# Diffusion backbone with routed experts: splits inside the rare branch, a sort spread over partitions, earlier transposes in experts, and ones multiplied during modulation

## The chip, the cores and the metric

The kernel runs on one core of a Trainium2 chip, which has engines that each run their own stream of instructions: TensorE (PE, matmuls), VectorE (DVE), ScalarE (ACT), GpSimd (POOL) and SyncE (SP, which issues most transfers). They wait for each other by semaphores. The metric is device time of one execution in microseconds (us); a number is the median of several executions.

## The reference

One layer of a hybrid backbone on 1024 tokens of width 1024: a modulation vector from the condition, a mixer (attention, recurrence, short convolution), and a mixture of 16 experts in which each token is routed to two. What bears on the change:

```python
mod = (cond @ w_ada[l] + b_ada[l]).reshape(bsz, N_MOD, 1, D_MODEL)
h = modulate(rms_norm(x, norm_mix_g[l]), mod[:, 0], mod[:, 1])
...
for e in range(N_EXPERTS):
    hid = jax.nn.silu(h @ w_gate[e]) * (h @ w_up[e])
    out = out + combine[..., e:e + 1] * (hid @ w_down[e])
```

Gate and up weights of an expert are 1024 x 512 each, the down weight 512 x 1024.

## The kernel before

**Precision.** Every float32 operand of a matmul is split into two parts of lower precision, `hi` (a cast by ACT) and `lo` (raw minus `hi`, by DVE), and a product is three matmuls (hi x hi, lo x hi, hi x lo). For a weight that is `Weights.split` (line 1756 for the DVE part, 1755 for ACT's): an expert's weights are 12 pieces of 128 x 1024, eight for gate and up (one for each 128 rows of the width) and four for down. `need(w, n)` splits until n pieces are done, `fill()` splits one more piece wherever it stands, up to 12 per expert and as far as buffers are free.

**Modulation at the start.** For j = 0 to 7 `weigh(j)` forms weighted sums of `w_ada` columns on ACT, DVE and POOL, and `total(j)` (lines 228 to 238) adds them up on PE: for each of two halves, two small matmuls on `wa` (line 233) and then two with ones on `mc` (line 235). `mods` reads the result on DVE (242, 244). `turn` transposes normalized tokens on PE (251), and ACT and DVE apply the modulation to them (254 to 256). `steps` (334) multiplies them by the input projection.

**Experts.** Tokens are sorted into lists in memory, one per expert. All experts have a first tile of 128 tokens (`Tile`, matmuls into `pg`). Experts 0 and 1 are taken in fixed places and are of kind "I": if they have more than 128 tokens, a branch (`tc.If(n > P)`, line 1591) runs `later`. The other 14 are sorted by their counts (`places`), and six of them, at places 2, 4, 6, 8, 10 and 12, are of kind "H" and have a half tile of 64 tokens besides (`Half`, `ph`). The rest have one tile. A few tokens beyond that are done in a tail.

The loop of one expert: `gate_up` for the first 4 of 8 slices of the width in both halves of the hidden width; the If of experts 0 and 1; the half tile's `gate_up`; the remaining slices; `act` (tanh on ACT, line 1364, and two operations on DVE, 1365 and 1366, make `t`); `Tile.turn`, which transposes `t` (PE 1389) and splits it into `hT` (ACT 1391, DVE 1392); transposes of the next expert's gathered tokens (`turn(xgs[0], 0)`, PE 1346, then ACT 92 and DVE 93 make `xT`); `down` (PE 1400); and `store`, in which DVE scales the result into `yt` (1405) for a scatter by POOL. The half tile does the same by lines 1414, 1416 (PE), 1427 (ACT), 1428 (DVE), 1438 (transposes on PE), 1441 (ACT), 1442 (DVE) and 1455.

**The order.** Each engine runs its instructions in the order in which this code issues them; nothing reorders them. So an operation on ACT or DVE stands behind all splits that `need` and `fill` put ahead of it. Memory in SBUF and PSUM is taken from pools with a fixed number of buffers: a new tile waits until the last reader of the old one is done.

Before the loop, expert 0's tokens come straight from PSUM (`xp`), are split into `xT` half by half, the lists of experts 0 and 1 are looked up by the ACT queue (`look`), and `places` sorts on one partition. In experts 0 and 1 all 12 pieces are split before the If, since both sides of it use them:

```python
                if KINDS[i] == "I":
                    need(w, 12)
                    with tc.If(n > P):
                        later(i, n, w)
```

Of the kernel before, what the change touches and what calls it, by code (L numbers as in the profile page):

```python
# [18 lines left out]
P = 128  # L19
D = 1024  # L20
# [14 lines left out]
C_ID, C_TRI, C_II, C_I16, C_GRP, C_E, C_TIE, C_POS, C_HALF, C_CAP, C_N = (  # L35
    0, 128, 256, 320, 336, 352, 368, 382, 396, 397, 411)
# [35 lines left out]
class Kernel:  # L72
# [84 lines left out]
    def start(self):  # L157
# [3 lines left out]
        with self.pool("xp", side="right") as xp:  # L161
# [46 lines left out]
            mt = [self.mo.tile([P, D], F32, name=c, bufs=n).rearrange("p (q i f) -> p q i f", i=2, f=P)  # L208
                  for c, n in (("macc", 1), ("mw", 2))]
# [18 lines left out]
            def total(j):  # L228

                pm = self.pmm.tile([P, 2, 2], F32, name="pm")  # L230
# [52 lines left out]
            for j in range(1, KD + 1):  # L283
                if 1 < j < KD - 2:
                    weigh(j + 2)
                if j < KD:
# [4 lines left out]
                if j == 1:  # L291
                    weigh(3)
                if j < KD:
# [30 lines left out]
    def steps(self, i, g, k0, k1):  # L324

        o, n = (0, 512, 1024)[g], (512, 512, 256)[g]
        if k0 == 0:
# [36 lines left out]
    def inproj(self, hc_es):  # L364
# [93 lines left out]
        def norm(ys, base):  # L458
# [8 lines left out]
            pn = self.pmm.tile([P, 8], F32, name="pm")  # L467
# [544 lines left out]
    def mixout(self):  # L1012
# [237 lines left out]
        V.tensor_copy(cn, pc[0:1, :])  # L1250
# [18 lines left out]
    def places(self, buf):  # L1269

        V, cst, cn, N = self.V, self.cst, self.cn, NE - 2
        dn, key, rk = (buf[0:1, 16 * i:16 * i + n] for i, n in enumerate((NE, N, N)))
        g1, g2 = (buf[0:1, i:i + N * N].rearrange("o (p e) -> o p e", e=N) for i in (256, 512))
        fix = lambda c: cst[0:1, c:c + N]
        inner, outer = (lambda x: x[:, None, :].to_broadcast([1, N, N])), (lambda x: x[:, :, None].to_broadcast([1, N, N]))
        V.scalar_tensor_tensor(out=key, in0=cn[:, 2:], scalar=16.0, in1=fix(C_TIE), op0=ALU.mult, op1=ALU.add)
        V.tensor_tensor(out=g1, in0=inner(key), in1=outer(key), op=ALU.is_gt)
        V.tensor_reduce(out=rk, in_=g1, axis=AX.X, op=ALU.add)
        V.tensor_tensor(out=g1, in0=inner(rk), in1=outer(fix(C_POS)), op=ALU.is_equal)
        V.tensor_tensor(out=g2, in0=g1, in1=inner(fix(C_I16 + 2)), op=ALU.mult)  # L1280
# [567 lines left out]
```

## Time and profile before

| | |
|---|---|
| median of 3 runs | 1118.6 us (1116.49 to 1125.67) |
| the profiled execution's own time | 1112.07 us |
| its span | 1110.3 us |
| PE busy | 1006.4 us (91%), 5242 instructions |
| DVE busy | 820.9 us (74%) |
| ACT busy | 592.5 us (53%) |
| POOL busy | 305.5 us (28%) |
| mean granted clock of PE | 0.977 |

The span is the profiled part of an execution. Busy is the time in which an engine executes; an engine waits for data in the rest, or has nothing to do. [...] The start (modulation) ends at about 75 us, and the experts run from 678 to about 1057 us.

### The profile page before, as it was taken

What the parts mean: (1) busy time and instruction counts of PE and PEld (TensorE: products, weight loads), DVE (VectorE), ACT (ScalarE), POOL (GpSimd) and SP (SyncE); (2) the same over time, 40 slices, a digit from 0 to 9 for tenths busy, and PEclk for the clock granted to TensorE, in tenths of its full rate; (3) what the DMA queues carried; (4) which work ended last, traced back from release to release, by engine and by line L of the source; (5) the groups of instructions that cost most, each with busy time, mean ns of one, the idle gap of its engine ahead of it and who ended that gap; (6) DMA issues with size and microseconds to landing.
All of it is one profiled execution on the core that took longest, in us unless ns stands there. A gap on an engine that the chain in (4) does not pass through costs nothing. (4 is left out here: it accounts for less than half of the span.)

```text
span 1110.3 us, 15751 instructions
## 1 busy us (share of the span) xinstructions
PE 1006.4 (91%) x5242; PEld 821.0 (74%) x5243; DVE 820.9 (74%) x1415; ACT 592.5 (53%) x964; POOL 305.5 (28%) x212
## 2 busy tenths in 40 slices
PE   2699999989999879998899996899999999999994
PEld 2577778878888779987788875677777777777773
DVE  5886897734563358887676777789797979889965
ACT  6674683432332358887422224567574756656751
POOL 3630012220001125245213233131323334131431
PEclk9999999989999989999999989899999999999997
DMA  9441434779444677775676747988998979898873
GB/s 326 137 124 61 144 93 120 260 258 311 143 133 120 176 192 197 239 204 191 249 265 226 275 143 270 362 273 270 308 293 272 326 247 340 236 351 246 286 254 133
DMA packets 139595, 251.21 MB, mean 226 GB/s; under 512 B 25283, under 2 KB 87205, under 8 KB 139460
## 3 DMA queue, kind: packets, MB, share of 16 engines
q1 hardware_dynamic: 130804, 228.13, 62.5%
q0 software_dynamic: 6736, 19.53, 7.4%
q10 hardware_dynamic: 1968, 2.47, 0.7%
q8 instruction: 45, 0.74, 0.3%
q14 instruction: 42, 0.34, 0.1%
HBM read 211.94 MB, written 45.55 MB: 232 GB/s over the span
## 5 line engine op out<-in xcount | busy, mean ns | idle before, releaser
L334 PE MATMUL ps<-h,block 128*128 128x512 f32 x1056 | 255.6, 398 | 2.1 <-DVE block L321 1.2
L334 PEld LDWEIGHTS ps<-h,block 128*128 128x128 f32 x1056 | 198.7, 191 | 44.1 <-DVE block L321 2.2
L1380 PE MATMUL pg<-q,xT 128*128 128x512 f32 x448 | 136.7, 398 | 3.4 <-DVE xT L93 2.7
L1380 PE MATMUL pg<-k,xT 128*128 128x512 f32 x320 | 112.3, 405 | 3.0 <-PEq L1591 2.8
L1336 POOL DMA_INDIRECT acc_d<-yt,recs x15 | 69.3, 4621 | 125.4 <-DVE yt L1405 125.4
L1380 PEld LDWEIGHTS pg<-q,xT 128*128 128x128 f32 x448 | 84.5, 189 | 24.6 <-DVE xT L93 2.8
L1756 DVE TENSOR_TENSOR q<-block,k 128x1024 fp32r<-128x1024 f32 x80 | 94.9, 1217 | 2.7 <-ACT k L1755 1.2
L1400 PE MATMUL py<-k,hT 128*128 128x512 f32 x204 | 81.2, 435 | 10.3 <-DVE hT L1392 4.2
L1755 ACT CAST k<-block 128x1024 fp32r<-128x1024 f32 x80 | 80.2, 1047 | 4.1 <-DMA recs<-list_d 3.8
L733 POOL TENSOR_TENSOR bt<-bt,mask 128x768 f32<-128x768 f32 x32 | 58.9, 1852 | 84.0 <-DMA bt<-b_d 83.9
L1380 PEld LDWEIGHTS pg<-k,xT 128*128 128x128 f32 x320 | 61.0, 191 | 17.5 <-issue 2.9
L782 ACT ACTIVATE sm<-sm,mx 128x640 f32<-128x640 f32 x64 | 53.2, 831 | 19.5 <-DVE mx L774 19.1
L796 DVE TENSOR_TENSOR p<-ps,p 128x640 fp32r<-128x640 f32 x64 | 52.6, 821 | 12.2 <-ACT p L795 12.1
L1400 PEld LDWEIGHTS py<-k,hT 128*128 128x128 f32 x204 | 40.0, 196 | 28.0 <-DVE hT L1392 10.7
L774 DVE CUSTOM_DVE_ANT_0 sm<-ps,bt 128x640 f32<-128x640 f32 x64 | 52.2, 817 | 9.8 <-PE ps L770 7.5
L770 PE MATMUL ps<-k,q 128*128 128x384 f32 (+1 forms) x256 | 52.6, 329 | 5.4 <-DVE q L703 2.2
L793 PE MATMUL ps<-cst,sm 128*128 128x128 f32 x320 | 47.0, 278 | 7.6 <-DVE mx L774 6.8
L520 DVE SCALAR_TENSOR_TENSOR macc<-mw,sil,macc 128x1024 f32<-128x1024 f32 x28 | 37.7, 1347 | 20.8 <-DMA mw<-in_w_ada_dram 20.6
L795 ACT CAST p<-ps 128x640 fp32r<-128x640 f32 x64 | 44.3, 692 | 16.1 <-PE ps L793 15.5
L1297 POOL DMA_INDIRECT block<-h_d,recs x21 | 26.3, 1252 | 94.5 <-PE pt L1346 75.8
L770 PEld LDWEIGHTS ps<-k,q 128*128 128x128 f32 x256 | 43.3, 194 | 7.4 <-issue 2.4
L98 POOL TENSOR_TENSOR ms<-ms,cst 128x1 f32<-128x1 f32 x26 | 17.5, 679 | 105.4 <-DVE ms L97 85.4
(373 smaller groups left out, 2278.3 us busy)
## 6 DMA issues: line engine op xcount, KB each, us to landing
block<-in_w_moe_dram SPq DMA_DIRECT2D x120, 512.0 KB
raw<-in_w_moe_dram SPq DMA_DIRECT2D x36, 512.0 KB
mw<-in_w_ada_dram SPq DMA_DIRECT2D x32, 512.0 KB
k<-in_w_moe_dram SPq DMA_DIRECT2D x24, 512.0 KB
bt<-b_d SPq DMA_DIRECT2D x30, 384.0 KB
block<-in_w_in_dram SPq DMA_DIRECT2D x22, 512.0 KB
wa<-in_w_ada_dram SPq DMA_DIRECT2D x16, 512.0 KB
block<-v_d SPq DMA_DIRECT2D x64, 128.0 KB
```

Of the source, the lines that this page charges most:

```text
L334: self.E.matmul(ps[:, 0:n], l[:, k, :], r[:, m, :], start=(k == 0 and q == 0), stop=(k == KD - 1 and q == 2))
L733: self.G.tensor_add(out=v, in0=v, in1=self.masks[n][:, g:g + 1].to_broadcast([P, 2, 384]))
L770: E.matmul(ps[:, dst], self.qs[i][h][:, it * P:(it + 1) * P], kv, start=(i == 0), stop=(i == 1))
L774: V.tensor_tensor_reduce(out=sm, in0=ps[:, all_], in1=self.bts[(u // 2) % 2][:, g, b0:b0 + 640], op0=ALU.add, op1=ALU.min, scale=-1.0, sca ...
L782: S.activation(sms[u, g], sms[u, g], AF.Exp, scale=-1.0, bias=mx, accum_out=lss[n][:, g, h:h + 1])
L793: E.transpose(pt[:, b * P:(b + 1) * P], sm[:, c:c + P], ident)
L796: return lambda: V.tensor_sub(pl, pt, ph.bitcast(F32))
L1336: nc.gpsimd.indirect_dma_start(out=acc_d, out_offset=bass.IndirectOffsetOnAxis(ap=rec[0:m, 1:2], axis=0), in_=y[0:m], in_offset=None, comp ...
L1380: E.matmul(self.pg[half], self.xT[x][:, k, :], self.w.gu(k, m, half), start=(k == 0 and i == 0), stop=(k == KD - 1 and i == 2))
L1400: E.matmul(self.py[c], hTs[x][:, f, :], self.w.dn(f, m, c), start=(f == 0 and i == 0), stop=(f == 3 and i == 2))
L1755: k.S.copy(hi, raw)
L1756: (eng or k.V).tensor_sub(lo, raw, hi.bitcast(F32))
```

## The change

- **Modulation.** A tile of ones (`one`, cast once by POOL) is multiplied by itself in `warm(n)`, matmuls whose result nobody reads: 8 in total(0) and 20 in total(1), between the `wa` and the `mc` matmuls of the first half, 5 ahead of the transposes of j == 1, 8 at j == 2. The PSUM tile `pm` becomes a whole bank.
- **Rare branch.** In experts 0 and 1 the If comes after 12 matmuls (first half, slices 0 to 3) and with 4 pieces split; `later` splits the other 8 for itself. On the usual side they are split where `fill` and `need` stand. Expert 0's two ACT copies now come ahead of both DVE subtractions, and its third terms stand last. In expert 1 the half transposes for `later` come ahead of the first matmuls.
- **Sort.** `places` works on 16 partitions, one per expert, in two parts with two small matmuls between; the first part runs in expert 0 ahead of `need(w, 8)`, the second after `act(1)`. The look at expert 2 follows it. Record loads of experts 0 and 1 go to POOL's queue.
- **Experts with a half tile.** `t.turn(1)` comes right after the half tile's first half; the next tokens are transposed in two groups of four with matmuls between; `t.store(c)` comes ahead of `h.turn(c)`.

```diff
+            def warm(n, t=None):
+                for _ in range(n):
+                    E.matmul(self.acc[0, 0] if t is None else t, one[:, 0:P], one[:, 0:512], start=True, stop=True)
...
+                    if i == 0:
+                        warm({0: 8, 1: 20}.get(j, 0))
...
+                if j == 1:
+                    warm(5)
...
+                if j == 2:
+                    warm(8, self.pmm.tile([P, 512], F32, name="pm"))
...
+        total = lambda x, y, out: V.tensor_tensor_reduce(out=sc, in0=x, in1=y, op0=ALU.mult, op1=ALU.add, scale=1.0, scalar=0.0, accum_out=out)
+        V.scalar_tensor_tensor(out=key, in0=self.lc[0:NE, 2:NE], scalar=16.0, in1=fix(C_TIE), op0=ALU.mult, op1=ALU.add)
+        total(key, fix(C_ID + 2), own)
+        V.tensor_tensor(out=sc, in0=key, in1=own.to_broadcast([NE, N]), op=ALU.is_gt)
+        V.tensor_reduce(out=rk, in_=sc, axis=AX.X, op=ALU.add)
+        V.tensor_scalar(oh, fix(C_POS), rk, None, op0=ALU.is_equal)
...
+        yield
+        pt = pst.tile([P, 512], F32, name="pt")[0:1]
+        E.matmul(pt[:, 0:N], cst[0:NE, C_IX:C_IX + 1], oh, start=True, stop=True)
+        E.matmul(pt[:, NE:2 * NE], dn, cst[0:NE, C_ID:C_ID + NE], start=True, stop=True)
...
-                    self.load(recs[:, i], lv[expert[i], :, 0:2], self.S if i < 2 else None)
+                    self.load(recs[:, i], lv[expert[i], :, 0:2], self.G if i < 2 else None)
...
+                done, m = list(w.parts), 12 - len(w.parts)
+                assert min(len(w.raw), len(self.his), len(self.los)) >= m
+                for hi, lo, raw in zip(self.his[:m], self.los[:m], w.raw):
+                    self.split(hi, lo, raw)
+                    w.parts.append((hi, lo))
...
                 if KINDS[i] == "I":
-                    need(w, 12)
+
+                    t.gate_up(0, 0, 4, not i)
                     with tc.If(n > P):
                         later(i, n, w)
+                    if not i:
+                        fill(2)
+                    gate_up(t, 1, 0, 4, 1 + (not i))
...
                 w.release(4)
+                if not i:
+                    order = self.places(yt, pst)
+                    next(order)
                 need(w, 8)
...
+                if not i:
+                    next(order, 0)
+                    look(2)
                 if half:
                     h.gate_up(0, 4)
+                    t.turn(1)
                     fill()
                 ahead(i + 2)
                 if i:
-                    x0 = turn(xgs[0], 0)
+                    x0 = turn(xgs[0], 0, (0,))
+                    if half:
+                        h.act(0)
+                        h.gate_up(1, 4, 6)
+                    turn(xgs[0], 0, (1,))
                     gather(rec(i + 2, 0), xgs[0]) if i + 2 < NE else None
                 if half:
-                    h.act(0)
-                    h.gate_up(1, 4)
+                    h.gate_up(1, 6)
                     fill()
-                    t.turn(1)
                     h.act(1)
...
                         t.down(c, 1)
+                        t.store(c)
                         h.turn(c)
-                        t.store(c)
```

Lines of the changed kernel stand 10 to 44 higher than those of before. Three places, each before and after.

DVE around the If of expert 0, before: after the end of the sort (1291 to 1293) come eight splits and the branch.

```order
L1293 CAST cnts<-yt 1x1
L1582 TENSOR_LOAD cnts
L1756 TENSOR_TENSOR q_4754<-block_5137,k_4753 128x1024
L1756 TENSOR_TENSOR q_4823<-block_5138,k_4822 128x1024
L1756 TENSOR_TENSOR q_4884<-block_5139,k_4883 128x1024
L1756 TENSOR_TENSOR q_4943<-block_5140,k_4942 128x1024
L1756 TENSOR_TENSOR q_4988<-block_5141,k_4987 128x1024
L1756 TENSOR_TENSOR q_5030<-block_4608,k_5029 128x1024
L1756 TENSOR_TENSOR q_5038<-block_4609,k_5037 128x1024
L1756 TENSOR_TENSOR lo<-block_4610,hi 128x1024
L1591 COMPARE_AND_BRANCH
```

After, behind the If: the last of four splits, the first part of the sort (1290 to 1295; two rows of 1290 make one operation), two splits and the first operation on `t`.

```order
L1802 TENSOR_TENSOR q_4986<-block_5183,k_4985 128x1024
L1291 SCALAR_TENSOR_TENSOR yt<-lc,cst 16x14
L1290 ISA yt<-yt,cst 16x14
L1290 ISA yt 16x1
L1293 TENSOR_TENSOR yt<-yt 16x14
L1294 TENSOR_REDUCE yt<-yt 16x1
L1295 TENSOR_SCALAR yt<-cst,yt 16x14
L1290 ISA yt<-yt,cst 16x14
L1290 ISA yt 16x1
L1802 TENSOR_TENSOR q_5031<-block_5184,k_5030 128x1024
L1802 TENSOR_TENSOR q_5073<-block_4651,k_5072 128x1024
L1386 SCALAR_TENSOR_TENSOR t_6302<-t_6302,pg_6359 128x256
```

The eight splits moved behind the branch; `t` stands behind six of them and the first part of the sort, where it stood behind all eight, two more and the whole sort.

PE in expert 2 (a half tile), before: the half tile's first half ends (`ph_7151`), then eight transposes of the next tokens and the second half (`ph_7160`); `t_6260`, the second half of the first tile, is transposed after it.

```order
L1414 MATMUL ph_7151<-q_4943,xT_6252 64x512
L1416 MATMUL ph_7151<-k_4942,xT_6252 128x512
L1346 MATMUL pt<-cst,block_5452 128x128 x8
L1414 MATMUL ph_7160<-q_4754,xT_6252 64x512
L1416 MATMUL ph_7160<-k_4753,xT_6252 128x512
L1414 MATMUL ph_7160<-q_4823,xT_6252 64x512
L1416 MATMUL ph_7160<-k_4822,xT_6252 128x512
L1414 MATMUL ph_7160<-q_4884,xT_6252 64x512
L1416 MATMUL ph_7160<-k_4883,xT_6252 128x512
L1414 MATMUL ph_7160<-q_4943,xT_6252 64x512
L1416 MATMUL ph_7160<-k_4942,xT_6252 128x512
L1389 MATMUL pt<-cst,t_6260 128x128 x2
```

After: the transposes of `t_6303` come first, those of the next tokens in two groups of four.

```order
L1441 MATMUL ph_7216<-k_4926,xT_6295 128x512
L1439 MATMUL ph_7216<-q_4986,xT_6295 64x512
L1441 MATMUL ph_7216<-k_4985,xT_6295 128x512
L1414 MATMUL pt<-cst,t_6303 128x128 x2
L1367 MATMUL pt<-cst,block_5495 128x128 x4
L1439 MATMUL ph_7225<-q_4797,xT_6295 64x512
L1441 MATMUL ph_7225<-k_4796,xT_6295 128x512
L1439 MATMUL ph_7225<-q_4866,xT_6295 64x512
L1441 MATMUL ph_7225<-k_4865,xT_6295 128x512
L1367 MATMUL pt<-cst,block_5495 128x128 x4
L1439 MATMUL ph_7225<-q_4927,xT_6295 64x512
L1441 MATMUL ph_7225<-k_4926,xT_6295 128x512
```

The two transposes of the first tile's `t` moved from behind the half tile's second half to the end of its first.

DVE a little further in the same expert, before: `t_6260` is the half tile's here, `hT_6258` its transposed form, `hT_6257` the first tile's, `yt` the store.

```order
L1756 TENSOR_TENSOR q_4681<-block_4608,k_4680 128x1024
L1392 SCALAR_TENSOR_TENSOR hT_6257<-pt,hT_6256 128x256
L1428 TENSOR_TENSOR ut<-ph_7160,ut 64x512
L1365 SCALAR_TENSOR_TENSOR t_6260<-t_6260,ut 64x256
L1366 TENSOR_TENSOR t_6260<-t_6260,ut 64x256
L1756 TENSOR_TENSOR q_4754<-block_4609,k_4753 128x1024
L1442 SCALAR_TENSOR_TENSOR hT_6258<-pt,hT_6258 128x2x64
L1405 SCALAR_TENSOR_TENSOR yt<-py,recs,row_6251 128x512
L1756 TENSOR_TENSOR q_4823<-block_4610,k_4822 128x1024
L1442 SCALAR_TENSOR_TENSOR hT_6258<-pt,hT_6258 128x2x64
L1405 SCALAR_TENSOR_TENSOR yt<-py,recs,row_6251 128x512
```

After:

```order
L1387 TENSOR_TENSOR t_6302<-t_6302,ut 64x256
L93 TENSOR_TENSOR xT_6297<-pt,xT_6293 128x512
L1802 TENSOR_TENSOR q_5489<-block_5182,q_5492 128x1024
L1453 TENSOR_TENSOR ut<-ph_7225,ut 64x512
L1386 SCALAR_TENSOR_TENSOR t_6303<-t_6303,ut 64x256
L1387 TENSOR_TENSOR t_6303<-t_6303,ut 64x256
L1802 TENSOR_TENSOR q_5490<-block_5183,q_5493 128x1024
L1430 SCALAR_TENSOR_TENSOR yt<-py,recs,row_6294 128x512
L1467 SCALAR_TENSOR_TENSOR hT_6301<-pt,hT_6301 128x2x64
L1802 TENSOR_TENSOR q_5491<-block_5184,q_5494 128x1024
L1430 SCALAR_TENSOR_TENSOR yt<-py,recs,row_6294 128x512
L1467 SCALAR_TENSOR_TENSOR hT_6301<-pt,hT_6301 128x2x64
```

`yt` now stands ahead of each `hT` of the half tile, and `hT` of the first tile is gone from this place: it stands earlier, right behind its `t`. One group of `xT` has come into this stretch.

## Rows read from the trace of the kernel before

**Rows 1.** The page: busiest engine; a group of instructions (busy us, mean ns)

```profile
PE 1006.4 (91%) x5242; PEld 821.0 (74%) x5243; DVE 820.9 (74%) x1415; ACT 592.5 (53%) x964; POOL 305.5 (28%) x212
...
L1755 ACT CAST k<-block 128x1024 fp32r<-128x1024 f32 x80 | 80.2, 1047 | 4.1 <-DMA recs<-list_d 3.8
```

**Rows 2.** Stretches: span; busy us of PE, PEld, DVE, ACT, POOL; PEclk, DMA share, GB/s

```profile
677.90:729.90 52.00, 43.46 (x184) 32.99 (x185) 44.47 (x64) 33.62 (x43) 9.41 (x6) 0.90 0.85 293
729.90:761.40 31.50, 30.58 (x137) 22.54 (x136) 25.04 (x35) 16.59 (x25) 10.93 (x4) 1.00 0.84 267
694.00:700.80 6.80, 5.45 (x15) 4.41 (x16) 5.69 (x9) 3.08 (x6) 0.00 (x0) 0.50 1.02 381
714.50:717.90 3.40, 3.20 (x8) 2.55 (x9) 2.14 (x2) 1.99 (x2) 0.00 (x0) 0.50 1.04 386
```

**Rows 3.** Waits of PE, 677 to 1060: total us, times, longest

```profile
PE pt L1389 <- DVE t L1366: 5.2, 1, 5.2
PE py L1400 <- DVE hT L1392: 4.2, 8, 0.8
PE py L1400 <- ACT hT L1391: 2.8, 6, 0.5
```

**Rows 4.** Timeline of PE, experts 0 and 1: start, duration, [idle before <-releaser]

```profile
695.35 0.66 PE L1389 MATMUL pt<-cst,t 128*128 128x128 f32 x2 [5.20 <-DVE t L1366]
...
705.49 2.26 PE L1380 MATMUL pg<-q,xT 128*128 128x512 f32 x9
...
714.70 0.76 PE L1380 MATMUL pg<-k,xT 128*128 128x512 f32 x1 [2.81 <-PEq L1591]
```

**Rows 5.** Timeline of DVE, expert 0

```profile
681.26 0.16 DVE L1289 SCALAR_TENSOR_TENSOR yt<-yt,lc 1x16 f32<-1x16 f32 x1
...
682.65 8.04 DVE L1756 TENSOR_TENSOR q<-block,k 128x1024 fp32r<-128x1024 f32 x7 [0.59 <-DVE cnts L1293]
...
694.79 0.42 DVE L1366 TENSOR_TENSOR t<-t,pg 128x256 f32<-128x256 f32 x1
```

**Rows 6.** Instructions of line 1591, the If: duration min/median/max, first and last start

```profile
L1591 PEldq COMPARE_BRANCH  x2: 3694/4725/5756, 679.4 to 708.8; - x2
```

**Rows 7.** Timeline of PE, expert 2 (half tile)

```profile
744.10 0.38 PE L1389 MATMUL pt<-cst,t 128*128 128x128 f32 x2
...
746.85 1.04 PE L1346 MATMUL pt<-cst,block 128*128 128x128 f32 x8
...
757.65 0.50 PE L1414 MATMUL py<-k,hT 128*128 128x512 f32 x1
```

**Rows 8.** Timeline of DVE, expert 2

```profile
744.93 0.42 DVE L1392 SCALAR_TENSOR_TENSOR hT<-pt,hT 128x256 fp32r<-128x256 f32 x1
...
746.08 0.42 DVE L1366 TENSOR_TENSOR t<-t,pg 128x256 f32<-128x256 f32 x1
746.57 1.23 DVE L1756 TENSOR_TENSOR q<-block,q 128x1024 fp32r<-128x1024 f32 x1
748.11 1.29 DVE L93 TENSOR_TENSOR xT<-pt,xT 128x512 fp32r<-128x512 f32 x2 [0.32 <-ACT xT L92]
...
756.12 0.28 DVE L1442 SCALAR_TENSOR_TENSOR hT<-pt,hT 128x128 fp32r<-128x128 f32 x1
756.32 0.74 DVE L1405 SCALAR_TENSOR_TENSOR yt<-py,recs,row 128x512 f32<-128x512 f32 x1
...
758.12 0.28 DVE L1442 SCALAR_TENSOR_TENSOR hT<-pt,hT 128x128 fp32r<-128x128 f32 x1
```

**Rows 9.** Timeline of PE, modulation

```profile
31.86 1.02 PE L235 MATMUL pm<-ones,mc 128*128 128x1 f32 x4 [6.67 <-DVE mc L221]
...
45.28 0.58 PE L235 MATMUL pm<-ones,mc 128*128 128x1 f32 x4
...
46.62 0.53 PE L251 MATMUL pt<-cst,x 128*128 128x128 f32 x3
```

**Rows 10.** Timeline of DVE, modulation

```profile
34.62 0.16 DVE L242 TENSOR_TENSOR md<-pm,vt 128x4 f32<-128x4 f32 x1 [2.69 <-PE pm L235]
```

More of the change, by code (lines that the diff above doesn't have):

```diff
@@ L466, in norm @@
                 yield 1
-            pn = self.pmm.tile([P, 8], F32, name="pm")
+            pn = self.pmm.tile([P, 512], F32, name="pm")[:, 0:8]
             for t in range(8):
@@ new lines, in places @@
+    def places(self, buf, pst):
+        V, E, cst, N = self.V, self.E, self.cst, NE - 2
+        key, sc, oh = (buf[0:NE, 16 * i:16 * i + N] for i in range(3))
+        own, rk, dn = (buf[0:NE, 48 + i:49 + i] for i in range(3))
+        fix = lambda c: cst[0:NE, c:c + N]
+        total = lambda x, y, out: V.tensor_tensor_reduce(out=sc, in0=x, in1=y, op0=ALU.mult, op1=ALU.add, scale=1.0, scalar=0.0, accum_out=out)
[4 more added lines that the diff above has]
+        V.tensor_scalar(oh, fix(C_POS), rk, None, op0=ALU.is_equal)
+        total(oh, fix(C_CAP), dn)
+        yield
+        pt = pst.tile([P, 512], F32, name="pt")[0:1]
+        E.matmul(pt[:, 0:N], cst[0:NE, C_IX:C_IX + 1], oh, start=True, stop=True)
+        E.matmul(pt[:, NE:2 * NE], dn, cst[0:NE, C_ID:C_ID + NE], start=True, stop=True)
+        V.tensor_copy(self.order[:, 2:], pt[:, 0:N])
+        d = buf[0:1, 64:64 + NE]
+        V.tensor_copy(d, pt[:, NE:2 * NE])
+        V.memset(d[:, 0:2], 2.0 * P)
+        V.tensor_copy(self.done, d)
+        V.scalar_tensor_tensor(out=d, in0=d, scalar=-1.0, in1=self.cn, op0=ALU.mult, op1=ALU.add)
+        V.tensor_scalar_max(d, d, 0.0)
+        V.tensor_copy(self.over, d)
+        V.tensor_reduce(out=own[0:1], in_=d, axis=AX.X, op=ALU.max)
+        V.tensor_copy(self.cnts[:, 2:], own[0:1])
@@ L1338, in scatter, with turn @@
                     in_=y[0:m], in_offset=None, compute_op=ALU.add)
-            def turn(xg, i):
+            def turn(xg, i, halves=(0, 1)):
                 xT = xTs[i]
-                for hh in range(2):
+                for hh in halves:
                     pt = pst.tile([P, 512], F32, name="pt")
@@ L1373, in __init__, with gate_up @@
                     self.pg = [None, None]
[L1375 removed]
+                def gate_up(self, half, k0=0, k1=KD, late=False):
                     if k0 == 0:
                         self.pg[half] = psg.tile([P, 512], F32, name=f"{self.name}{half}")
[L1378 to L1381 removed]
+                    jobs = [(k, i) for k in range(k0, k1) for i in range(3)]
+                    if late:
+                        jobs.sort(key=lambda j: j[1] == 2)
+                    for q, (k, i) in enumerate(jobs):
+                        x, m = TERMS[i]
+                        E.matmul(self.pg[half], self.xT[x][:, k, :], self.w.gu(k, m, half),
+                                 start=(k0 == 0 and q == 0), stop=(k1 == KD and q == len(jobs) - 1))
                 def act(self, half):
@@ L1579, in experts @@
                 half = KINDS[i] == "H"
[L1580 removed]
+                if i:
+                    look(i + 2)
                 if KINDS[i] == "I":
```

77 lines of the change are left out of this document (28 added, 49 removed).

## The prediction

> **What bounds the kernel now.** I read the profile in this order. The page first: TensorE (PE) is busy for 91% of the span [rows 1], so a gain has to close one of its gaps, and what makes it wait costs the full amount. The stretches next: the first two experts take 52.00 us, of which PE is busy 43.46, and an expert with a half tile takes 31.50 us with PE busy 30.58 and VectorE (DVE) 25.04 [rows 2]. Then the list of waits inside the expert loop: one wait of 5.2 us for `t`, eight for `hT` on DVE (4.2 us), six for `hT` on ScalarE (ACT) [rows 3]. The reader should see there that the gaps are few and that DVE or ACT ends nearly all of them: in the expert loop PE does not wait for weights from memory.
>
> The first two experts hold the big gaps: 5.20 us at 695.35 and 2.81 us at 714.70 [rows 4]. After both the granted clock is 0.50, for 6.8 and 3.4 us [rows 2]. The rows show the first gap's cause: DVE does ten splits in a row from 682.65 and reaches the second operation on `t` at 694.79 [rows 5]. The second is PE's own branch at the If: 3694 ns in expert 0, where it hides behind matmuls, and 5756 in expert 1 [rows 6].
>
> **The start.** Before, PE comes back at 31.86 to finish total(1), and DVE can go on only at 34.62: 2.76 us. The same twelve small matmuls take from 45.28 to 46.62, 1.34 us, once PE runs at full clock [rows 9, 10]. The change puts 20 matmuls of 512 columns into the 6.67 us wait ahead. At half clock one takes 0.43 us (8 in 3.40 us) [rows 2], so all 20 would take 8.5 us and end 1.9 us late; if the clock rises in the middle of them, 12 cold and 8 at about 0.23 (137 in 30.58) [rows 2] take 7.0 us, 0.3 late, and the tail then saves 1.4. That gains 1.1. The eight in total(0) and their effect on its transposes may gain 0 to 1.0 more (DVE waits little there), the five at j == 1 stand in front of transposes that ACT nearly waits for and cost 0 to 2.1 (5 x 0.43). I take a gain of 0.7, bounds a gain of 2.5 and a loss of 2. After 35 us DVE is what the loop waits for, so the rest of the ones multiplied buy nothing.
>
> **Experts 0 and 1.** The rare branch now has its own splits, so only four pieces are split ahead of the If instead of twelve, and the sort is 8 short rows on 16 partitions and later 9 more; a row of that size on one partition takes 0.16 [rows 5], with the pause to the next about 0.19. I followed the new order by hand with the durations of the rows: a split costs DVE 1.15 us, a pair on `t` 0.9 [rows 8]. PE starts at 677.7, at best 0.2 earlier than now, because its PSUM bank is free only after both subtractions. It does 12 matmuls (2.8 us) and passes the If at about 680.7; the first cast behind the If waits for that, so DVE starts splitting at 681.9, as early as before less 0.75. Four splits, the first sort (1.1 to 1.5), two splits, then `t`: done at 691.1 where it was 695.21. The 5.20 us wait becomes 1.8. But the splits that were done ahead are late next: in front of the second `hT` of expert 0 now stand a split, the second sort (1.8), and three more splits, which makes PE wait some 3.5 us near 699. In expert 1 the If stays: PE's sequencer met the branch at 708.8 [rows 6], 3.3 us after the expert began at 705.49 [rows 4], with 10 of 24 matmuls and 8 short transposes still to run, so it looks some 18 ahead; the 12 matmuls and 8 transposes that stand there after the change are no longer cover than that, and a branch of 5.76 leaves a hole of about 2.5, and six splits that cannot start before PE is through it cost another 1.3 at the turn of `t`. Summed: 1.8 + 3.5 + 2.5 + 1.3 + 0.9 of short ones = 10.0 us of waits, where before there were 5.2 + 2.8 + 0.9 of short ones. Before, the half clock came on top: 6.8 + 3.4 us at half rate, 3.3 us of lost work as far as PE was busy in them. By waits alone expert 2 starts 0 to 1 us later; with no half clock at all 3.3 us are won. I expect half of those spells again and take a gain of 1.3, bounds a gain of 5 (branch at its shorter 3.7, no half clock) and a loss of 1.5.
>
> [...] The row says 5756 ns on PE [rows 6], and I go by the row.
>
> **Experts with a half tile (six).** The change removes two waits per expert, 0.47 and 0.45 us (the six on ACT's `hT` and six of the eight on DVE's) [rows 3]: `t.turn(1)` comes before the transposes of the next expert's tokens. That is 0.92 us. But it moves work on DVE and ACT too, and here I think it loses. Take the expert that begins at 729.93 [rows 7, 8]:
> - DVE ends the second `t` at 746.50 and goes straight on to a split at 746.57. Now `hT` comes first on both ACT and DVE. PE reaches the transposes at 746.85 as before; from the first turn of this expert DVE starts `hT` 0.83 us after PE starts transposing (744.10 to 744.93), so at 747.68. DVE idles 1.2 us.
> - The next cast on ACT (1.05 us) [rows 1] stands behind ACT's part of `hT`, from about 747.25, and so ends at about 748.65. DVE idles another 0.65 after its `hT`. Of this idle time some 0.3 was there before (748.11). Net 1.5 us later. What follows (`ut`, `t`, halves of `xT`, splits) is the same work in another order, without gaps to absorb it: two waits of 0.5 for tanh remain.
> - `t.store` now comes before `h.turn`: DVE does `yt` (0.66 from start to start) ahead of each `hT` of the half tile. Before, that `hT` began at 756.12. Now 756.12 + 1.5 + 0.66 = 758.3, done 758.55.
> - PE comes to the half tile's down matmuls at 757.65 - 0.92 = 756.73, and waits 1.85. The second `hT` follows the first by a split, `yt` and itself, 2.0 us; PE's fifth matmul there wants it four matmuls or 1.0 after the first and waits 1.0.
> Sum: 1.85 + 1.0 - 0.92 = 1.93 us lost; the transposes of the second `t` half may wait 0 to 0.6 for the same late chain. I take 2.0 per expert, bounds 1.5 and 2.3, so 12 for six.
>
> The other eight experts keep their order, and DVE has five pieces of lead there instead of eleven; the first piece not split ahead is wanted 6.4 us in and ready at about 4.1, so I cost it at nothing. Moving record loads to POOL's queue and the look at expert 2 later costs nothing as long as PE's waits in the loop name no transfer, as now [rows 3].
>
> **Sum.** -0.7 - 1.3 + 12.0 = +10.0 us. On the profiled execution 1112.07 gives 1122.1. The median of the runs stands 6.5 above it (1118.6), so I forecast 1128, 0.9% slower, just inside what a measurement of this kernel can tell from no change (about 1%).
>
> **Rivals.**
> - *The half tile's waits also drop the clock.* The 2.81 us gap brought 3.4 us at half rate [rows 2, 4]. The new waits come as up to 0.6, 1.85 and 1.0 within some 4.5 us, less idle time in one piece. A spell costs 1.7 us. It decides from three of six experts on: +5 to +10, 1133 to 1138, clearly slower. Chance 0.2. [...]
> - *`hT` is not late*, because DVE has slack in these experts (25.04 of 31.50 us busy) and catches up. Then 0.92 x 6 = 5.5 are gained: -0.7 - 1.3 - 5.5 = -7.5, 1111. Against it: the slack lies in waits for PE and ACT, and the chain from 746.50 to 758.12 has little of it. Chance 0.1, a third of it with the head's larger gain too, under 1107.
> - *The head and the start give all they can*: -5 - 2.5 + 9 = +1.5, 1120. Chance 0.08.
>
> **How the numbers follow.** My forecast has 0.62; its own range, from the bounds of the terms, is 1120 to 1134, and two fifths of it lie above 1129.8, the mark of 1%. Slower: 0.25 + 0.2 = 0.45. Faster (under 1107.4): 0.03 to 0.04. Within 1%: 0.51. The range that leaves out 2 in 10 reaches to the first rival's 1138 and down to 1116.
>
> **What would show it.** Right: in the six experts, waits at the half tile's down matmuls (line 1414 and 1416 of before) that end on DVE's `hT`, about 1.9 and 1.0 us, with 33.4 to 33.6 us per such expert instead of 31.50; in expert 0 a wait of about 1.8 us for `t`; a wait of 2.5 at the second If; total(1) over in 1.4 us. Wrong: 30.6 us per half-tile expert (the second rival), or the stretch from expert 0 to expert 2 under 47 us, or half clock inside the half-tile experts.

## The result and the profile after

| | before | after |
|---|---|---|
| median | 1116.65 us (20 runs, 1112.41 to 1125.67) | 1124.46 us (20 runs, 1121.33 to 1128.74) |
| ratio, 95% interval | | 1.0066 (1.0052 to 1.0081) |
| profiled execution's own time | 1112.07 us | 1121.72 us |
| PE busy | 1006.4 us | 1020.3 us |

The forecast was 1128 us, 0.9% slower, with a range of 1120 to 1134. The changed kernel is 0.66% slower: its interval leaves out no change, but it lies inside the 1% that the forecast took as its mark. Between the two profiled executions the forecast was +10.0 us, and +9.65 were measured. Three terms of that sum were off, and they cancelled. Lines of the changed kernel stand up to 46 higher than those of before (1756 is now 1802). Where the time went is read from the starts of the stages on PE:

| | before | after | difference |
|---|---|---|---|
| last matmul of the modulation on `wa` begins | 84.62 | 84.0 | -0.6 |
| expert 0 begins | 677.89 | 678.99 | +1.1 |
| expert 0 to expert 2 | 52.04 | 45.92 | -6.1 |
| six experts with a half tile, summed | 189.14 | 204.98 | +15.8 |
| expert 14 begins | 1036.42 | 1046.17 | +9.75 |

The experts with one tile shorten by 0 to 0.3 us each, 1.1 in all. Between 84 and 678 us, where the change touches nothing, 1.7 us went lost (593.3 us before, 595.0 after); in the other executions below that stretch takes 593.1 to 598.5 us, so nothing is read from it.

The page's first part, and three stretches (span; busy us of PE, PEld, DVE, ACT, POOL with instructions; granted clock as a share of PE's full one, DMA share, GB/s): experts 0 and 1, the first expert with a half tile, and the fourth one.

```profile
PE 1020.3 (91%) x5287; PEld 833.3 (74%) x5288; DVE 820.6 (73%) x1415; ACT 590.7 (53%) x964; POOL 324.1 (29%) x215
```

```profile
678.90:724.90 46.00, 40.20 (x188) 29.94 (x189) 38.87 (x61) 30.68 (x40) 10.56 (x8) 1.00 0.84 286
724.90:758.70 33.80, 31.65 (x138) 23.59 (x137) 24.97 (x35) 16.35 (x25) 12.91 (x4) 0.95 0.83 269
...
885.70:918.90 33.20, 30.49 (x138) 22.69 (x137) 24.96 (x35) 16.43 (x25) 12.97 (x4) 1.00 0.79 257
```

Beside [rows 2]: the first stretch had 0.90 as its clock and has 1.00, and PE's idle time in it falls from 8.5 us (52.00 - 43.46) to 5.8. The expert with a half tile went from 31.50 to 33.80 us, with about the same work of DVE (25.04, now 24.97). Its clock is 0.95 in five of the six; in the fourth expert it stays 1.00, and that one takes 33.20.

The waits of PE in the expert loop (total us, times, longest), beside [rows 3]:

```profile
PE py L1439 <- DVE hT L1467: 10.5, 6, 1.8
PE pt L1367 <- DVE hT L1417: 2.7, 1, 2.7
PE pg L1405 <- DVEq L1622: 2.6, 1, 2.6
PE pt L1414 <- DVE t L1387: 2.5, 2, 1.5
PE pt L1463 <- DVE t L1387: 2.4, 6, 0.4
PE py L1441 <- DVE hT L1467: 2.4, 5, 0.6
```

The six waits of 0.47 for ACT's `hT` are gone. In their place stand the first, the fifth and the last line: 15.3 us, all at the half tile's `t` and `hT`. (The third line is the start of expert 0, where before had 2.7 us too, ended by DVE's `xT`.) The timeline of PE at the first of these places (start, duration, idle before and its releaser), and of DVE in the same expert:

```profile
751.42 0.31 PE L1463 MATMUL pt<-cst,t 64*128 64x64 f32 x2 [0.39 <-DVE t L1387]
753.48 0.80 PE L1439 MATMUL py<-k,hT 128*128 128x512 f32 x1 [1.75 <-DVE hT L1467]
```

```profile
737.61 0.42 DVE L1386 SCALAR_TENSOR_TENSOR t<-t,pg 128x256 f32<-128x256 f32 x1 [4.19 <-ACT t L1385]
...
742.71 0.42 DVE L1417 SCALAR_TENSOR_TENSOR hT<-pt,hT 128x256 fp32r<-128x256 f32 x1 [1.21 <-ACT hT L1416]
743.64 1.23 DVE L1802 TENSOR_TENSOR lo<-block,hi 128x1024 fp32r<-128x1024 f32 x1 [0.51 <-ACT hi L1801]
...
752.48 0.75 DVE L1430 SCALAR_TENSOR_TENSOR yt<-py,recs,row 128x512 f32<-128x512 f32 x1
753.14 0.28 DVE L1467 SCALAR_TENSOR_TENSOR hT<-pt,hT 128x128 fp32r<-128x128 f32 x1
```

DVE has the two holes that the forecast worked out, 1.2 and 0.65 us, here 1.21 and 0.51; after them it stops only twice, 0.48 us each, for ACT's tanh, up to the `hT` at 753.14 for which PE stands still, with `yt` just ahead of it. The 4.19 us in which DVE does nothing before the first `t` will matter below. After the waits the clock falls, to 0.64 over these 4 us:

```profile
752.00:756.00 4.00, 2.52 (x6) 1.68 (x7) 4.00 (x7) 1.65 (x3) 0.50 (x1) 0.64 0.59 175
```

The If, for which [rows 6] showed 3694 and 5756 ns on PE, and what PE's gaps are in expert 0 (the one at 692.24 was 5.20 in [rows 4]):

```profile
L1622 PEldq COMPARE_BRANCH  x2: 323/338/352, 679.1 to 703.5; - x2
```

```profile
682.17 2.33 PE L1405 MATMUL pg<-q,xT 128*128 128x512 f32 x9 [0.15 <-PEq L1622]
...
692.24 0.41 PE L1414 MATMUL pt<-cst,t 128*128 128x128 f32 x2 [1.45 <-DVE t L1387]
...
699.90 0.66 PE L1367 MATMUL pt<-cst,block 128*128 128x128 f32 x4 [2.75 <-DVE hT L1417]
```

So the hole behind the branch, a term of the sum, has all but gone. The diff moves the If, but nothing in it sets out to shorten the branch.

### The profile page after: what moved, and what is told of

The parts are those of the page before. It is cut to its first block, busy times and chain, and to the rows that moved or that the text cites. A ratio compares the mean times of both kernels' runs of the same rounds, so it can differ in the third digit from the quotient of the medians.

```text
span 1119.9 us, 15852 instructions
## 1 busy us (share of the span) xinstructions
PE 1020.3 (91%) x5287; PEld 833.3 (74%) x5288; DVE 820.6 (73%) x1415; ACT 590.7 (53%) x964; POOL 324.1 (29%) x215
## 5 line engine op out<-in xcount | busy, mean ns | idle before, releaser
L1357 POOL DMA_INDIRECT acc_d<-yt,recs x15 | 76.9, 5124 | 123.0 <-DVE yt L1430 64.8
L1405 PE MATMUL pg<-k,xT 128*128 128x512 f32 x320 | 110.0, 399 | 0.0
L1425 PE MATMUL py<-k,hT 128*128 128x512 f32 x204 | 76.4, 416 | 5.9 <-DVE yt L1729 2.6
L1385 ACT ACTIVATE t<-pg 128x256 f32<-128x256 f32 x32 | 12.3, 384 | 74.2 <-PE pg L1405 74.1
```

The source lines that it names most:

```text
L1357: nc.gpsimd.indirect_dma_start(out=acc_d, out_offset=bass.IndirectOffsetOnAxis(ap=rec[0:m, 1:2], axis=0), in_=y[0:m], in_offset=None, comp ...
L1405: E.matmul(self.pg[half], self.xT[x][:, k, :], self.w.gu(k, m, half), start=(k0 == 0 and q == 0), stop=(k1 == KD and q == len(jobs) - 1))
L1425: E.matmul(self.py[c], hTs[x][:, f, :], self.w.dn(f, m, c), start=(f == 0 and i == 0), stop=(f == 3 and i == 2))
```

## The experiments

Each is compared with runs of the kernel before on the same chip (medians 1114.85 to 1116.84); ratios are against those, with the 95% interval.

### Which part of the expert's order costs the time

**The changed kernel without its order in half-tile experts** (both edits taken back):

```diff
                 if half:
                     h.gate_up(0, 4)
-                    t.turn(1)
                     fill()
...
-                    x0 = turn(xgs[0], 0, (0,))
-                    if half:
-                        h.act(0)
-                        h.gate_up(1, 4, 6)
-                    turn(xgs[0], 0, (1,))
+                    x0 = turn(xgs[0], 0)
...
-                    h.gate_up(1, 6)
+                    h.act(0)
+                    h.gate_up(1, 4)
                     fill()
+                    t.turn(1)
...
-                        t.store(c)
                         h.turn(c)
+                        t.store(c)
```

> The changed kernel with the order of the half-tile experts put back to that of before (transposes of the second t behind the half tile's second half, next tokens transposed in one group of eight, h.turn ahead of t.store); the start, the rare branch and the sort stay changed. Theory (the new order makes DVE late with hT of the half tile, and the waits drop the clock): the six half-tile experts go back to 31.5 us each from 33.2 to 34.8, no half clock in them, about 14 to 15 us less than the changed kernel, that is 5 to 7 us under the kernel before. Rival (the experts are slower because DVE now has 5 pieces of lead where it had 11): they stay above 33 us and the time stays about 8 us above before.

Measured: 1108.6 us, 0.9941 (0.9917 to 0.9965). The waits are those of before again:

```profile
PE py L1425 <- DVE hT L1417: 4.2, 8, 0.8
PE py L1425 <- ACT hT L1416: 2.8, 6, 0.5
```

and these experts take 31.53 to 31.56 us. So the rest of the change gains 0.6%, and the order in six experts loses 1.25% (1.0066 - 0.9941), some 14 us.

**The order alone, put into the kernel before** (the same edits the other way).

> The kernel before with only the order of the half-tile experts changed (early transposes, next tokens in two groups, t.store ahead of h.turn). Theory (that order alone makes DVE late, whatever the lead of splits): half-tile experts of 33.2 to 34.8 us as in the changed kernel, 13 to 16 us above before, 1.2 to 1.4%. Rival (it needs the smaller lead that the new rare branch leaves): experts of 31 to 32 us and at most 3 us above before. PE's branch at the If takes 3.7 and 5.8 us as in the kernel before, since nothing ahead of it changes.

Measured: 1129.77 us, 1.0125 (1.0078 to 1.0173): the same 1.25% from the other side. The six take 34.21, 34.75, 33.19, 34.29, 34.74 and 33.19 us. There are two lengths: 33.2, as in the expert above whose clock stayed 1.00, and 34.2 to 34.8.

**One of the two edits at a time.** First `h.turn(c)` ahead of `t.store(c)` again, the early transposes kept; then the old place of the transposes, `t.store(c)` ahead kept.

```diff
                         t.down(c, 1)
-                        t.store(c)
                         h.turn(c)
+                        t.store(c)
```

> The changed kernel with h.turn ahead of t.store again; the early transposes stay. Theory, worked out from the order and the durations of the trace: of 2.1 us lost in waits per half-tile expert 0.7 goes, because yt no longer stands ahead of hT, so 4 us less than the changed kernel by waits alone and up to 7 if the clock drops in fewer experts: 1 to 4 us above before. Rival (the store is the whole loss): experts of 30.6 to 31.5 us, 5 to 10 us under before.

Measured: 1120.72 us, 1.0045 (1.0022 to 1.0067); half-tile experts of 32.5 to 34.1 us. The second wait is gone. At the place of the first stands one of the same length, but now it ends with `yt`:

```profile
PE py L1439 <- DVE yt L1430: 11.1, 6, 1.8
PE pt L1463 <- DVE t L1387: 2.4, 6, 0.4
```

> The changed kernel with the transposes of the second t and of the next tokens in the order of before; only t.store stays ahead of h.turn. Theory: the two old waits of 0.47 and 0.45 return, the wait at the half tile's down matmuls shrinks to about 0.8 in all, experts of about 32.0 to 32.2 us, 9 to 12 us less than the changed kernel: 1 to 4 us under before. Rival (the store is the whole loss): experts of 33 us and more, still 5 to 8 us above before.

Measured: 1113.25 us, 0.997 (0.9949 to 0.999); 31.82 to 31.90 us per expert. So `yt` ahead of `hT` costs 0.35 us by itself, and the early transposes cost 1.0 to 2.6 by themselves. With them and without `yt` ahead PE still waits 1.8 us at the first down matmul. That matmul needs both: `hT` to read, and one of the two PSUM buffers `py`, which is free only when `yt` has read it. Whichever of the two DVE does last ends the wait, so the order of the pair can't shorten it, and the theory of 0.7 us for it failed: what is late is the whole chain, not the last link.

**The early transposes with the splits placed for them.** Theory: the transposes themselves are no loss; they bring `hT` to DVE at a moment at which its next splits were queued behind, while DVE idled 4.19 us ahead of the first `t`. Rival: DVE and ACT have too much to do in this pair of tiles, so that any earlier `hT` only moves the wait.

```diff
-                gate_up(t, 0, 4, 8, 4 if half else 2)
+                gate_up(t, 0, 4, 8, 1 if half else 2)
...
-                    t.turn(1)
                     fill()
+                    t.turn(1)
...
                     h.gate_up(1, 6)
-                    fill()
...
-                        fill()
+                        fill(1 - c)
                         t.down(c, 1)
-                        t.store(c)
                         h.turn(c)
+                        t.store(c)
```

(`fill` splits one piece after each slice instead of one after four; fewer pieces remain for later.)

> The changed kernel, its early transposes kept, but with a split ahead of them instead of behind, no split between the half tile's second half and down, one fewer between the down matmuls, h.turn ahead of t.store, and the splits taken out done earlier, in the four slices ahead of the first t, where DVE sat idle for 2.5 us. Theory (these experts are bound by the order on DVE, not by its amount of work): no wait at the half tile's down matmuls, half-tile experts of 30.0 to 30.2 us, about 8 us less than with the old order: 13 to 15 us under before, about 1.2%. Rival (DVE's amount of work bounds a pair of experts, so that what is won in one is lost in the next): the half-tile expert is shorter and the one after it longer by the same, no gain over the old order.

Measured: 1100.06 us, 0.9855 (0.9815 to 0.9894). The stretch of the first half-tile expert, and DVE at the first `t`:

```profile
727.70:757.80 30.10, 30.10 (x138) 22.74 (x137) 26.19 (x36) 17.66 (x26) 16.61 (x4) 1.00 0.90 301
```

```profile
740.37 0.42 DVE L1386 SCALAR_TENSOR_TENSOR t<-t,pg 128x256 f32<-128x256 f32 x1 [0.77 <-ACT t L1385]
```

PE is busy for all 30.10 us, with DVE busier than before (26.19). The rival falls: 4.19 us of idle time became 0.77, filled with splits, and both waits that the change set out from and both that it made are gone. That is 1.4 us per expert under the kernel before, where the order as written cost 2.64.

### What shortened experts 0 and 1

Two theories: the eight splits put inside the rare branch, which DVE no longer does ahead of the If; or PE's branch, 0.34 us instead of 3.7 to 5.8. First, how much there is to explain: the profiles hold the same code for these two experts in six kernels with the short branch. The change, the one with `h.turn` ahead and the one with the ones moved (below) take 45.9 us, at a clock of 1.00. The three others (the order taken back, the transposes taken back, the splits placed) take 48.75 to 48.97 us, at 0.93 and 0.94. The first of these three:

```profile
682.35:731.10 48.75, 43.02 (x189) 32.09 (x189) 38.94 (x61) 30.68 (x40) 10.53 (x8) 0.94 0.81 276
```

So of the 6.1 us gained some 3 come and go with the clock between executions, and 3.1 stand in all six.

**The splits ahead of the If again**, in the changed kernel:

```diff
                     t.gate_up(0, 0, 4, not i)
+                    need(w, 12)
                     with tc.If(n > P):
```

> The changed kernel with all 12 pieces of experts 0 and 1 split ahead of the If again (the sort, the early If, the queues and the rest stay). Theory (t of expert 0 no longer stands behind ten splits, that is the gain of the head): PE's wait for the first t goes from 1.45 back to some 3.5 to 4 us and the stretch from expert 0 to expert 2 from 46 to 48 to 50 us, 2 to 4 us above the changed kernel. Rival (the gain is PE's branch of 0.3 us in place of 5.8): no change against the changed kernel, under 1 us.

Measured: 1121.5 us, 1.0047 (1.0023 to 1.0071), and 44.4 us for experts 0 and 1 where the change has 45.92. PE's longest waits there:

```profile
PE pt L1414 <- DVE t L1387: 1.7, 1, 1.7
PE pt L1367 <- DVE hT L1417: 1.5, 1, 1.5
```

The wait for `t` becomes 0.3 longer, the one for `hT` 1.2 shorter, and the one of 1.0 at the turn of `t` in expert 1 is gone. So the splits in the branch gain nothing; by the profiles they cost 1.5 us or more, and the runs do not contradict it (the intervals of the two ratios overlap). What, then, brought the wait for the first `t` from 5.2 us to below 2? DVE's splits in expert 0, with the splits ahead of the If and in the change:

```profile
680.90 8.04 DVE L1803 TENSOR_TENSOR q<-block,k 128x1024 fp32r<-128x1024 f32 x7
```

```profile
683.27 4.63 DVE L1802 TENSOR_TENSOR q<-block,k 128x1024 fp32r<-128x1024 f32 x4 [4.43 <-ACT k L1801]
```

PE begins this expert at 680.98 and 678.99. In the first kernel DVE splits from PE's start on, where before it began 4.8 us after it (682.65 against 677.89), with the sort ahead [rows 5]; `t` is done 14.0 us after PE's start instead of 17.3. So by the profile it is the sort, gone from ahead of the splits, that shortened this wait; no run moves the sort alone. In the second, the change, the first cast stands behind the If, and DVE does nothing for 4.43 us.

**The ones alone, put into the kernel before; and the changed kernel without them.** 41 matmuls more, or fewer, far from the experts.

```diff
             def warm(n, t=None):
-                for _ in range(n):
+                for _ in range(0 * n):
```

> The kernel before with only the ones multiplied during modulation. Theory: total(1) ends in 1.3 us instead of 2.7, the 20 matmuls end within 0.5 us of the moment at which the wait ended before, and the stretch to 75 us is 0.3 to 1 us shorter: no difference that can be told in the whole. Besides, it moves the If by 41 matmuls in PE's code and leaves the rare arm as it was: if the place in the code made PE's branch take 3.7 and 5.8 us, it takes another time here (0.3 as in the changed kernel, or more); if the arm's content or what stands around it did, it stays at 3.7 and 5.8 us.

> The changed kernel without the ones multiplied (41 matmuls left out, the tiles stay). Theory: DVE goes on 1 to 1.5 us later after total(1), and most of it is lost again by 75 us; 0 to 1 us above the changed kernel, not to be told from it. Rival (the start carries 2 us or more to the end): 2 us and more above. PE's branch at the If: the 41 matmuls ahead of it are gone, so its time tells with the run before whether the place in the code decides.

Measured: 1110.02 us, 0.995 (0.9925 to 0.9974) with the ones alone; 1132.9 us, 1.0133 (1.0073 to 1.0193) without them. The ones are worth 0.5 to 0.7%, where both theories had put their gain at 1 us or less. And the branch follows them (first the kernel before with them, then the change without them):

```profile
L1605 PEldq COMPARE_BRANCH  x2: 352/386/421, 686.2 to 714.7; - x2
```

```profile
L1622 PEldq COMPARE_BRANCH  x2: 4621/5348/6076, 683.0 to 711.4; - x2
```

```profile
717.63 2.34 PE L1405 MATMUL pg<-q,xT 128*128 128x512 f32 x9 [2.73 <-PEq L1622]
```

Without the ones the hole of "about 2.5" is there, with 2.73 us, and experts 0 to 2 take 52.46; with them in the kernel before, 48.33. How can a matmul at 15 us change a branch at 700? It stands ahead of it in PE's code: each is two instructions, a load and a multiplication (the page counts 5242 multiplications and 5243 loads before, 5283 and 5284 with the 41 ones).

**Only the place in the code.** Matmuls of two columns into a part of `pm` that is overwritten (work added, nothing left out) stand in total(0) and total(1) of the kernel before, 20 and 21 of them; then 20 in total(1) alone.

```diff
             def total(j):
...
+                for _ in range({1: 20}.get(j, 0)):
+                    E.matmul(pm[:, 1, :], was[j][:, KV, 1, :], sil[:, KV::KD], start=True, stop=True)
```

> The kernel before with 41 matmuls of 2 columns more on PE, in the waits of total(0) and total(1), whose results are overwritten: as many instructions ahead of the If as in the changed kernel, but little for the clock. Theory (the place in PE's code decides how long the branch takes): the branch takes 0.3 to 0.5 us instead of 3.7 to 6, the stretch from expert 0 to expert 2 some 48 us instead of 52, and the modulation is as slow as without the ones: 3 to 4 us under before. Rival (the clock or the time at which PE gets there decides): 3.7 to 6 us again, and no difference to before.

> The kernel before with 20 small matmuls of 2 columns, results overwritten, in the wait of total(1) alone. In the run with 41 each ran as two passes, took 0.21 us and so made the start late by some 6 us. 20 take 4.3 of a wait of 6.7 us, so the start is as before, and they shift PE's code ahead of the If by 80 instructions, as the change does. Theory (the place in the code makes the branch long): the branch takes 0.3 to 0.5 us, the stretch from expert 0 to expert 2 is 48 us instead of 52, the whole 3 to 5 us under before, a ratio of 0.996 to 0.997. Rival (something else of the change or of the larger padding made it short): 3.7 to 6 us and a ratio of 1.000.

Measured: 1116.63 us, 1.0013 (0.9981 to 1.0044), and 1113.4 us, 0.9973 (0.9957 to 0.999). Each product is two matmuls here: 40 matmuls and 40 loads more in the second. In both the branch is short, and experts 0 and 1 take 47.95 and 48.11 us:

```profile
L1593 PEldq COMPARE_BRANCH  x2: 327/340/353, 688.0 to 717.3; - x2
```

```profile
L1593 PEldq COMPARE_BRANCH  x2: 327/340/353, 686.0 to 714.2; - x2
```

The first missed the gain expected because its 41 products held the modulation up by about 6 us. In the second the 40 matmuls took 8.5 us, not the 4.3 expected, and made total(1) some 1.7 us longer than without them (11.9 us from its first matmul to its last, before 10.2). It shows the effect of the place alone: 80 instructions more in PE's code, and two experts are 4 us shorter and the time 0.27%. PE reaches the first transposes of `t` as late as before (17.45 us after the expert's start, before 17.46); the hole of 2.81 us and the half clock behind it are gone.

| kernel | PE instructions of ones or products added ahead | PE's branch, ns |
|---|---|---|
| before; order alone; change without ones | 0 | 3694 to 6076 |
| before with 20 small products | 80 | 327, 353 |
| before with ones; change; ones moved (below) | 82 | 323 to 445 |
| before with 41 small products | 164 | 327, 353 |

The change's own order moves its If too: 12 matmuls of its expert stand ahead of it instead of 24, and the sort has put four small ones between. By the code that is 24 instructions fewer ahead in expert 0 and 16 fewer in expert 1. So the long branch came at shifts of 0, -24 and -16 (3694 to 6076 ns), the short one at shifts of 58 to 164 (323 to 446 ns).

**What else the ones do.** The eight at j == 2 are moved into the earlier waits, so that their count stays:

```diff
-                        warm({0: 8, 1: 20}.get(j, 0))
+                        warm({0: 12, 1: 24}.get(j, 0))
...
-                if j == 2:
-                    warm(8, self.pmm.tile([P, 512], F32, name="pm"))
```

> The changed kernel with the 8 matmuls of ones at j == 2 moved into the two earlier waits (12 and 24 there instead of 8 and 20): the same number of instructions, so that the If stays at its place. Theory (those 8 fill the wait of 2.5 to 3.5 us near 50 us and so keep the clock up while PE has most to do, 50 to 65 us): the clock of that stretch is near 0.5 again and modulation ends 2 to 3.5 us later: 2 to 3 us above the changed kernel. Rival (the ones in total(1) are what counts, by ending it 1.4 us sooner): within 1 us of the changed kernel.

Measured: 1127.16 us, 1.0108 (1.0073 to 1.0144), 0.4% over the change (the two intervals overlap a little), with the branch short (335 and 445 ns). Stretch 50 to 65 us of the change, of the change without ones, and with the eight moved:

```profile
50.00:65.00 15.00, 13.13 (x85) 11.36 (x86) 14.40 (x31) 9.84 (x19) 6.35 (x8) 1.00 0.28 82
```

```profile
50.00:65.00 15.00, 12.77 (x47) 11.33 (x48) 12.48 (x25) 8.74 (x15) 6.33 (x8) 0.52 0.26 78
```

```profile
50.00:65.00 15.00, 13.06 (x48) 11.57 (x49) 12.50 (x25) 8.74 (x15) 6.32 (x8) 0.52 0.24 71
```

Where the eight are missing PE is busy nearly as long and does 47 and 48 matmuls instead of 77 (85 less the eight): at half clock PE is what the loop waits for (DVE stands 2.0 us for `pm` there in both, in the change not at all), and the last `wa` matmul begins at 87.16 and 86.94 instead of 84.0. The eight do not decide the clock alone. The profiled execution of before happened to have 0.89 in this stretch; the order alone, whose code is the same up to the experts, had 0.54. It was 0.83 in the profile of the ones alone and 1.00 in three more with the eight in place (the change, the splits ahead of the If, the best of both below), and 0.52 to 0.89 in six without them.

### The best of both

Early transposes with the splits placed for them, and the splits of experts 0 and 1 ahead of the If.

> The order that won 1.45% (a split ahead of the early transposes, three splits done earlier), with all 12 pieces of experts 0 and 1 split ahead of the If as in the kernel before. Theory (the splits inside the rare branch cost time when it is not taken, since they make hT of expert 0 late: 44.4 against 45.9 us from expert 0 to expert 2 in the profiles): 1 to 3 us under that version, 1098 to 1100, 1.6% under before. Rival (that difference is the chance of the clock): no difference to it.

Measured: 1097.88 us, 0.9845 (0.9798 to 0.9891): the fastest, 1.5% under the kernel before. How much the second edit adds to the first can't be told from the intervals.

## Why the prediction came out, point by point

**The half-tile experts: right in place and mechanism, the term too small.** The step said +2.0 us per expert, by 1.85 at the first down matmul, 1.0 at the fifth and 0.92 saved. The profile of the fourth expert has 1.75 there, 0.57 at the fifth, 0.40 ahead of both at the transposes, and 0.92 saved: 1.8 net, against 33.2 - 31.5 = 1.7. The other five carry the first rival on top: a lower clock after the waits (0.60 to 0.79 over 4 us), 0.6 to 1.6 us each. "It decides from three of six experts on": it was five of six. In the profile the term is 14.8 (15.84 less the 1.07 won in one-tile experts), in the runs 1.25% or 14 us, not 12. The step also gave `yt` ahead of `hT` 0.66 us of the first wait; alone it costs 0.35, and without it that wait is 1.8 all the same. The size came out because the matmul waits for `yt` in either order, which the step did not see: before, `yt` ended at 757.06 [rows 8], and 1.5 later than that is 1.83 after 756.73.

How little idle time is enough for the clock to fall, the rows of before don't show. The trace now has waits after which it fell in one expert and not in another: after 0.39, 1.75 and up to 0.57 us it fell in five experts (in the first already within the 1.75); in the fourth, with the same three, 0.40, 1.75 and 0.57, it did not. With the order alone two of six kept it (33.19 us). So these waits alone do not decide it.

**The second rival fell, and fell usefully.** "`hT` is not late" did not happen: PE waits 1.75 us. But its premise, that DVE has slack, was right. The slack stood ahead of the first `t`, where the order did not use it; moving splits there gave 30.10 us, under the 30.6 which the text named as this rival's mark.

**Experts 0 and 1: the step failed.** Forecast a gain of 1.3, bounds -5 and +1.5; measured 6.1, under the mark of 47 us that the text itself set as wrong (3.1 in the three other profiles of the same code, 48.75 to 48.97 us). What failed is the sentence that the If stays as it is in expert 1 and "a branch of 5.76 leaves a hole of about 2.5". I took the branch's time for a property of the branch; it is one of its place in PE's code, 0.32 to 0.45 us instead of 3.7 to 6.1 in the profiles with 58 to 164 instructions more ahead. The waits for DVE were forecast well: 1.8 (measured 1.45) for `t`, 3.5 (2.75) for `hT`, 1.3 (1.01) at the turn of `t` in expert 1. The change without the ones is the case that the step worked out: those three waits were 1.46, 2.73 and 1.01, the hole 2.73, and the stretch 52.46 us, 0.4 over before, inside the step's bounds. Of the 6.5 us between that kernel and the change 2.6 are the hole. The other 4.0 are PE's busy time at a lower clock (44.16 us against 40.20):

```profile
682.90:686.30 3.40, 3.36 (x8) 2.72 (x9) 0.00 (x0) 0.00 (x0) 1.54 (x2) 0.50 0.54 149
...
706.00:710.00 4.00, 3.66 (x12) 3.10 (x13) 3.66 (x5) 2.48 (x3) 1.01 (x1) 0.57 1.04 379
```

These two spells, at the first expert's start and behind its wait for `hT`, lie ahead of the hole, and the change has the same waits there at a clock of 1.00. The three profiles of 48.75 to 48.97 us have the short branch and a clock of 0.93 and 0.94; in the first of them it is 0.84 from 682 to 692 us and 0.86 from 700 to 712, around the same two places, and 1.00 between them. So the branch explains the hole; the clock at these two places is not the branch's doing, and 6.1 holds a favourable execution. Why it stays up in some executions is open. That the wait for `t` would shrink came true, by the profile through the sort; the splits inside the rare branch, which the step put beside it, cost 1.5 us or more.

For the branch the prediction went by the row, 5756 ns on PE [rows 6]. The changed kernel has 323 and 352 ns for its two, so the row did not hold; in the change without the ones, at 4621 and 6076, it did, about.

**The start: the size failed.** Total(1) is over in 1.4 us as forecast, and `md` at 32.92 where it was 34.62 [rows 10]; the 20 matmuls took 7.17 us (forecast 7.0 to 8.5). But "After 35 us DVE is what the loop waits for, so the rest of the ones multiplied buy nothing" was read from an execution whose clock was 0.89 there. At 0.52, which the experiments found without the ones, PE is what the loop waits for, and the eight at j == 2 are worth about 0.4%, though the intervals overlap a little.

**Why the total held.** By luck: +12 became +14.8, -1.3 became -6.1, and the start and the stretch behind it gave +1.1 for -0.7. The errors of +2.8, -4.8 and +1.8 cancel, and +9.8 stands against +10.0 (+9.65 over the whole execution). The margin of 6.5 us from profile to median was too large. It rested on three runs; twenty give a median of 1116.65 and a margin of 4.6, and 2.7 for the change: the profile of before was a favourable execution, 0.4% under the median of its runs, that of the change only 0.2% under. The bounds of the terms, added up, reach to 1136 and not to 1134; the measured 1124.46 lies inside either.

**What stays open.** That 80 instructions turn a branch of 5 us (3694 and 5756 ns) into one of 0.34 (327 and 353) is shown; why they do is not, and no run here shows what PE does in those 5 us. Shifts of 58 to 164 did equally well; which others would, no run tells.

## What to carry to other kernels

Moving an operation earlier on PE brings its followers on ACT and DVE forward in their queues too: write down what then stands behind them, and move that work into the idle time that the trace shows earlier, else the wait only changes its place. A long branch in a row may belong to its place in the code: when an edit adds instructions anywhere ahead, its row of before need not hold after (3694 and 5756 ns became 327 and 353 with 80 more), and padding is a cheap trial. Before calling an engine's slack harmless, look at the clock of that stretch in more than one execution (here 0.89 and 0.54 for the same code).

## What the runs showed of the hardware

- The same If takes PE's queue 0.32 to 0.45 us or 3.7 to 6.1 us, with the number of PE instructions ahead of it (long in three profiles with none added or 16 to 24 fewer, short in nine with 58 to 164 more); on the other engines' queues it stays at 45 to 72 ns, with the ones and without them.
- Matmuls whose results nobody reads paid here: with eight in a wait of the modulation the clock from 50 to 65 us was 0.83 to 1.00 in four profiles, without them 0.52 to 0.89 in six. Moving them away cost 0.4%, 4.7 us by the ratios, with intervals that overlap a little.
- Waits of 0.4, 1.75 and up to 0.6 us close together cost more than their sum here: in five experts of six the clock fell (0.60 to 0.79 over the 4 us behind them), and they took 33.8 to 34.8 us in place of 33.2.
